# A PSUM bank of its own for the dilated attention's norm and transpose products, inside a recurrence stage

## The chip, the cores and the metric

The kernel runs on one core of a Trainium2 chip. The metric is the device time of one execution in microseconds; three runs of the kernel before gave a median of 2457.34 us (2457.04 to 2457.57). The core has five engines with a queue each, worked off in order: TensorE (PE, with its weight loads PEld), VectorE (DVE), ScalarE (ACT), GpSimd (POOL) and SyncE (SP), which here issues the DMAs. PSUM, where PE's products land, has eight banks of 128 partitions x 512 fp32 values.

## The reference

Two blocks on 512 tokens of width 1024. The first: x plus half a SwiGLU, then a mixer, then again half a SwiGLU. The mixer projects the normed x to an RWKV-7 branch, a dilated attention branch and two gates:

```python
p_rwkv, p_q, p_k, p_v, p_gate = _split_last(h @ w_in[l], (RWKV_COLS, ATTN_WIDTH, ATTN_WIDTH, ATTN_WIDTH, N_BRANCHES * D_MODEL))
y_a = rwkv7_time_mix(p_rwkv, ...)
y_b = dilated_attention(p_q, p_k, p_v, attn_q_norm[l], attn_k_norm[l])
g_a, g_b = _split_last(jax.nn.sigmoid(p_gate + b_gate[l]), (D_MODEL, D_MODEL))
merged = g_a * (y_a @ w_proj_rwkv[l]) + g_b * (y_b @ w_proj_attn[l])
x = x + merged @ w_out[l]
```

The RWKV branch is a recurrence over the tokens in 16 heads of 64, `state = state * w_t + (state @ a_t) b_t + v_t k_t`, with out = state @ r_t. The dilated attention has 12 heads in three groups; q and k are RMS-normed per head before it:

```python
q = rms_norm(heads(pq), q_gain) * (HEAD_DIM ** -0.5)
k = rms_norm(heads(pk), k_gain)
v = heads(pv)
```

The second block (two layers of a hybrid of MLA, GQA and a convolution, with a context) is not touched by the change.

## The kernel before, in words

Everything is fp32. A weight product is three matmuls over split operands (`mm3`, L623: whi*HH, whi*HL, wlo*HH); ACT makes whi from the DMA'd raw weights and DVE makes wlo (`wsplit`, L583). One 128 x 512 output tile over 8 k-slices is thus 24 matmuls into one PSUM bank, called prj in the stage below.

The change lies in the recurrence's stage, `rwkv` (L1185). There five streams of work run beside each other:

- `rw_chunks` (L1449), for each of 8 head pairs j, 8 chunks of 64 tokens one after the other. A chunk: po = AA x SV (PE, rows 0 to 63 and 64 to 127), copy pp <- po (ACT), pu = TB x pp (PE), copy SV <- pu (ACT), pS = Bt x SV (PE), a second product into po's rows 64 to 127 (PE), the state of the next chunk SV <- se + pS (DVE), and copy Og <- po (ACT), the chunk's output. After the eighth chunk a tail (`rw_tail`, L1496) norms the pair's output, with PE products py and pgg.
- `rw_solve` (L1403): for pair j the inverse of triangular blocks. AS is loaded from DRAM, 31 steps run on DVE (tiles pr and Tt), the result goes through DRAM into TB, DVE transposes AS <- TB, then PE products pZ and pW, and ACT copies TB <- pW. With that copy pair j's chunks may take pu. AS has one buffer.
- `rw_prep` (L1275): for pair j the decays, keys and the tiles AA, BB, Bt, SV. It has 13 PSUM tiles: pz, pa, pl, psk, prn, four of pA, pb, pv, two of pbt. Its tile AA has two buffers, so that DVE's AA <- pA for pair j waits for the last chunk of pair j-2.
- `rw_stream` (L1247): r, k and v projections, three prj tiles a pair, at most two pairs ahead.
- `rw_fill` (L1261): the attention's 18 q, k, v tiles (`qkv_steps`, L992), then 16 gate tiles. Each attention tile starts a chain (`qkv_chain`, L999): ACT copies fq <- prj (and, for q and k, squares it), which frees prj's bank. For q and k, PE makes ssq, the sums of squares; ten small DVE operations make the reciprocal root (dqx, dqi, drk, dqt); for k, ACT spreads it out, PE transposes it into bcq and DVE multiplies; the result is stored by qkT <- fq. For v, PE transposes into pt, ACT copies it and it is stored by vd <- fq. Only one chain is let in at a time (`qch`), and prj has two banks.

PSUM in this stage: pools "mm" (prj, 2 banks), "g" (2), "u" (pZ, pW, py, pgg; 1), "po" (2) and "us" (pu, pS; 1). All eight banks are in use.

The order of the work comes out of two steps. `drive` (L440) records which stream goes on next, by a clock with assumed durations, in which a tile waits for the earlier tile in its buffer (`alloc`, L295). Then the framework orders each engine's instructions by priority, which is the recorded order with shifts (`RW_LATE`, `RW_AHEAD`, L19 and L20: the chain's instructions come earlier, the projections' later, and twelve prj matmuls in a row stay together), hands out the buffers and sets the waits.

Of the kernel before, what the change touches and what calls it, by code (L numbers as in the profile page):

```python
# [7 lines left out]
F32 = mybir.dt.float32  # L8
# [5 lines left out]
P = 128  # L14
# [425 lines left out]
def drive(k, tasks):  # L440

    clk, plan, flags = k.clk, k.plan, k.flags
    live = {}
    n = 0

    def hint(x, y):
        x[3] = None
        if isinstance(y, tuple):  # L450
            x[3], y = y[:2], y[2]
        x[2] = clk.last
        if y.startswith("+"):
            y, x[2] = y[1:], 0.0
        x[5] = y.startswith("w")
        x[4] = y.lstrip("w")

    k.born = list(tasks)
    while live or k.born:
        for prio, y, g in k.born:  # L460
            live[n] = x = [prio, g, 0.0, None, "PE", False]
            hint(x, y)
            n += 1
        k.born = []
        if plan.recording:
            best = None
            for i, x in live.items():
                if x[5] and k.held:
                    continue
                r = x[2]  # L470
                if x[3] is not None:
                    w = flags.get(*x[3])
                    if w is None:
                        continue
                    r = max(r, w)
                s = clk.soon(x[4], r) + x[0]
                if best is None or s < best[0]:
                    best = (s, i)
            assert best is not None, ("tasks wait for one another", [(x[1].gi_code.co_name, x[3:]) for x in live.values()])
            i = best[1]  # L480
            plan.steps.append(i)
        else:
            i = plan.steps[plan.si]
            plan.si += 1
        x = live[i]
        assert x[3] is None or flags.get(*x[3]) is not None, "order of tasks"
        clk.last = 0.0
        late = k.late.get(x[1].__name__, 0)
        k.tc._tc.cur_priority += late
        try:  # L490
            y = next(x[1])
        except StopIteration:
            del live[i]
            continue
        finally:
            k.tc._tc.cur_priority -= late
        hint(x, y)
# [32 lines left out]
class K:  # L530
# [468 lines left out]
    def qkv_chain(self, g, u, i, p, k):  # L999
        nc, t1 = self.nc, self.t1  # L1000
        c = self.take("qch")
        yield self.need("qch", c, "ACT")
        v = p.rearrange("p (b t) -> p b t", b=4) if g == 0 else p.rearrange("p (t b) -> p b t", b=4)
        q = t1.tile([P, 4, P], F32, tag="fq0", name="fq0")
        nc.scalar.copy(q, v)
        if u == 2:
            self.free("rwmm", k)
            yield "PE"
            pt = self.rps["g"].tile([P, 4, P], F32, tag="g", name="pt")
            for b in range(4):  # L1010
                nc.tensor.transpose(pt[:, b], q[:, b], self.ident)
            yield "ACT"
            vt = t1.tile([P, 4, P], F32, tag="fq1", name="fq1")
            nc.scalar.copy(vt, pt)
            nc.sync.dma_start(self.vd[g][:, :, i * P:(i + 1) * P], vt)
            self.free("qch", c)
            return
        sq = t1.tile([P, 4, P], F32, tag="fq1", name="fq1")
        nc.scalar.square(sq, v)
        self.free("rwmm", k)  # L1020
        if u == 0:

            nc.sync.dma_start(self.qkT[g, 0][:, i], q.rearrange("p b t -> p (b t)"))
        yield "PE"
        ss = self.rps["g"].tile([P, 8], F32, tag="g", name="ssq")
        for b in range(4):
            nc.tensor.matmul(ss[:, 2 * b:2 * b + 2], sq[:, b], self.rcon["bd"][:, 0:128:64], start=b == 0, stop=True,
                             skip_group_check=True)
        yield "DVE"
        r = self.sm.tile([P, 8], F32, tag="drk", name="drk")  # L1030
        self.rstd(r, ss, 1.0 / 64, 1e-6, "dq")
        if u == 0:
            nc.vector.tensor_copy(self.RQ[:, g, :, 2 * i:2 * i + 2], r.rearrange("p (b h) -> p b h", h=2))
            self.free("qch", c)
            return
        yield "ACT"
        rnb = sq.rearrange("p b (h d) -> p (b h) d", d=64)
        nc.scalar.copy(rnb, r.unsqueeze(2).to_broadcast([P, 8, 64]))
        yield "PE"
        bc = self.rps["g"].tile([P, 4, P], F32, tag="g", name="bcq")  # L1040
        for b in range(4):
            nc.tensor.transpose(bc[:, b], sq[:, b], self.ident)
        yield "DVE"
        nc.vector.scalar_tensor_tensor(q, q, self.gg, bc, ALU.mult, ALU.mult)
        nc.sync.dma_start(self.qkT[g, 1][:, i], q.rearrange("p b t -> p (b t)"))
        self.free("qch", c)
# [138 lines left out]
    def rwkv(self, H, ya, tw, lad, gd):  # L1185
        nc, tc = self.nc, self.tc
        with ExitStack() as ctx:
            E = ctx.enter_context
            cp = E(tc.tile_pool(name="rc", bufs=1))
            self.t1 = E(tc.tile_pool(name="r1", bufs=1))  # L1190
            self.t2 = E(tc.tile_pool(name="r2", bufs=2))
            self.rps = {t: E(tc.tile_pool(name="rp" + t, bufs=b, space=PSUM))
                        for t, b in (("mm", 2), ("g", 2), ("u", 1), ("po", 2), ("us", 1))}
            self.scrA = [tc.dram_tile([2, 16, 32, 32], F32, name=f"scrA{j}") for j in range(8)]
            self.scrT = [tc.dram_tile([2, 16, 32, 32], F32, name=f"scrT{j}") for j in range(8)]
            self.rw = [dict() for _ in range(8)]
            o = PAR_COLS["a0"][0]
            self.a0h = cp.tile([P, 8], F32, name="a0h")
            nc.vector.tensor_scalar_mul(self.a0h, self.par_t[:, o:o + 8], 0.5)
            o = PAR_COLS["b_gate"][0]  # L1200
            self.bgh = cp.tile([P, 16], F32, name="bgh")
            nc.vector.tensor_scalar_mul(self.bgh, self.par_t[:, o:o + 16], 0.5)

            def seq(f, *a):
                s = (y for j in range(8) for y in f(j, *a))
                s.__name__ = f.__name__
                return s

            self.nb["rwmm"], self.nb["qch"] = 2, 1
            self.late = RW_LATE  # L1210
            drive(self, [
                (0, "PE", seq(self.rw_chunks, ya, gd)),
                (300, "PE", seq(self.rw_solve)),
                (600, "PE", seq(self.rw_prep, tw, lad)),
                (RW_PRIO["stream"], "PE", self.rw_stream(H)),
                (RW_PRIO["fill"], "PE", self.rw_fill(H)),
            ])
            self.late = {}
# [1290 lines left out]
```

## Time and profile before

| | |
|---|---|
| median of 3 runs | 2457.34 us |
| the profiled execution | 2463.02 us, its span 2461.2 us |
| PE busy, weight loads | 95%, 78% of the span |
| DVE, ACT, POOL busy | 70%, 41%, 8% |
| mean granted TensorE clock | 0.955 |
| the recurrence's stage | 392 to 1061 us of the span |

The profile is of one execution. Times count from the span's start. A tile is named by the program's name without its buffer number; "out<-in" says what an instruction writes and reads. PE's ends are modelled, so its starts are the better guide. Nearly all instructions carry the line of one recording helper (L320), so that they are told apart by their tiles. The granted clock is a share of full speed: 1.0 is 2.4 GHz, 0.5 is 1.2 GHz, and a figure between is a mixture over time.

### The profile page before, as it was taken

What the parts mean: (1) busy time and instruction counts of PE and PEld (TensorE: products, weight loads), DVE (VectorE), ACT (ScalarE), POOL (GpSimd) and SP (SyncE); (2) the same over time, 40 slices, a digit from 0 to 9 for tenths busy, and PEclk for the clock granted to TensorE, in tenths of its full rate; (3) what the DMA queues carried; (4) which work ended last, traced back from release to release, by engine and by line L of the source; (5) the groups of instructions that cost most, each with busy time, mean ns of one, the idle gap of its engine ahead of it and who ended that gap; (6) DMA issues with size and microseconds to landing.
All of it is one profiled execution on the core that took longest, in us unless ns stands there. A gap on an engine that the chain in (4) does not pass through costs nothing.

```text
span 2461.2 us, 33891 instructions
## 1 busy us (share of the span) xinstructions
PE 2347.4 (95%) x12556; PEld 1913.8 (78%) x12556; DVE 1733.4 (70%) x3620; ACT 1017.3 (41%) x1852; POOL 198.8 (8%) x202
## 2 busy tenths in 40 slices
PE   8999999999999999989989999999899999899997
PEld 7888887777777777758878888888778777678776
DVE  8888867675577656546668755656679976689866
ACT  4222234333333233345344542334446555355553
POOL 0000000011011110000001000000021210121110
PEclk9999999998799779989999999999999999899998
DMA  6545542333223224433333333243310222211121
GB/s 221 176 171 171 179 164 94 92 96 95 77 70 98 62 56 125 140 111 110 121 104 118 96 118 92 92 146 121 127 58 25 81 66 95 90 47 48 54 76 51
DMA packets 122199, 254.26 MB, mean 103 GB/s; under 512 B 39209, under 2 KB 54577, under 8 KB 121393
## 3 DMA queue, kind: packets, MB, share of 16 engines
q1 hardware_dynamic: 122032, 252.09, 32.5%
q8 instruction: 99, 1.62, 0.3%
q14 instruction: 68, 0.55, 0.1%
HBM read 222.07 MB, written 21.59 MB: 99 GB/s over the span
## 4 chain that ended last, share of the span: by engine, by line
PE 82%; DVE 9%; issue 3%; ACT 3%; POOL 2%; DMA 1%; SPq 0%; POOLq 0%; DVEq 0%; ACTq 0%
PE po L320 14%; PE prj L320 13%; PE pu L320 11%; PE pg L320 10%; PE pj L320 8%; PE pm L320 5%; PE pwo L320 4%; PE sc L320 2%; PE pt L320 2%; PE pA L320 2%; DVE X L320 1%; PE pkv L320 1%; PE pl L320 1%; PE ss L320 1%; DVE wlo L320 1%
## 5 line engine op out<-in xcount | busy, mean ns | idle before, releaser
L320 ACT CAST whi<-wraw 128x1024 fp32r<-128x1024 f32 (+4 forms) x330 | 324.9, 985 | 674.4 <-PE po L320 136.0
L320 DVE TENSOR_TENSOR wlo<-wraw,whi 128x512 fp32r<-128x512 f32 (+7 forms) x627 | 421.8, 694 | 103.1 <-ACT whi L320 92.5
L320 PE MATMUL prj<-HH,whi 128*128 128x512 f32 x464 | 199.3, 430 | 0.0
L320 PE MATMUL prj<-HH,wlo 128*128 128x512 f32 x464 | 192.5, 415 | 0.0
L320 PE MATMUL prj<-HL,whi 128*128 128x512 f32 x464 | 189.4, 408 | 0.0
L320 PE MATMUL pg<-HH,whi 128*128 128x512 f32 x352 | 139.2, 395 | 7.7 <-ACT HH L320 6.8
L320 PE MATMUL po<-FH,whi 128*128 128x512 f32 x352 | 139.0, 396 | 0.0
L320 PE MATMUL po<-FL,whi 128*128 128x512 f32 x352 | 139.0, 395 | 0.0
L320 PE MATMUL po<-FH,wlo 128*128 128x512 f32 x352 | 138.9, 395 | 0.0
L320 PE MATMUL pu<-HH,whi 128*128 128x512 f32 x352 | 138.7, 394 | 0.2 <-ACT whi L320 0.2
L320 PE MATMUL pg<-HL,whi 128*128 128x512 f32 x352 | 138.2, 393 | 0.0
L320 PE MATMUL pu<-HL,whi 128*128 128x512 f32 x352 | 137.5, 391 | 0.0
L320 PE MATMUL pu<-HH,wlo 128*128 128x512 f32 x352 | 135.0, 390 | 0.0
L320 PE MATMUL pg<-HH,wlo 128*128 128x512 f32 x352 | 134.9, 390 | 0.0
L320 PE MATMUL pj<-HH,whi 128*128 128x512 f32 (+1 forms) x304 | 124.6, 413 | 3.2 <-ACT HH L320 3.2
L320 ACT ACTIVATE pr<-sc,am 128x768 f32<-128x768 f32 (+1 forms) x120 | 97.9, 816 | 64.1 <-DVE am L320 58.3
L320 PE MATMUL pj<-HL,whi 128*128 128x512 f32 (+1 forms) x304 | 123.5, 407 | 0.0
L320 PE MATMUL pj<-HH,wlo 128*128 128x512 f32 (+1 forms) x304 | 122.0, 402 | 0.0
L320 DVE TENSOR_TENSOR ptl<-pt,pth 128x512 fp32r<-128x512 f32 x156 | 104.8, 683 | 23.1 <-ACT pth L320 21.5
L320 ACT CAST pth<-pt 128x512 fp32r<-128x512 f32 x156 | 89.6, 586 | 57.5 <-PE pt L320 56.7
L320 DVE TENSOR_REDUCE am<-sc 128x1 f32<-128x768 f32 (+1 forms) x120 | 100.6, 843 | 16.1 <-PE sc L320 15.6
L320 PEld LDWEIGHTS prj<-HH,whi 128*128 128x128 f32 x464 | 91.9, 198 | 23.3 <-issue 5.0
(745 smaller groups left out, 5633.1 us busy)
## 6 DMA issues: line engine op xcount, KB each, us to landing
wraw<-in_ffn_w SPq DMA_DIRECT2D x96, 512.0 KB, 3.4
wm<-in_l_mod SPq DMA_DIRECT2D x48, 512.0 KB, 4.4
wraw<-in_l_b SPq DMA_DIRECT2D x45, 512.0 KB, 3.3
wraw<-in_w_rkv SPq DMA_DIRECT2D x24, 512.0 KB, 4.1
wraw<-in_w_qkv SPq DMA_DIRECT2D x18, 512.0 KB, 3.4
wraw<-in_w_gate SPq DMA_DIRECT2D x16, 512.0 KB, 3.8
wraw<-in_ffn_w SPq DMA_DIRECT2D x16, 448.0 KB, 3.5
xd<-X SPq DMA_DIRECT2D x24, 256.0 KB, 2.1
```

Of the source, the lines that this page charges most:

```text
L320: r = real(*a, **kw)
```

## The change

The chain's three PSUM tiles go from pool "g" to a new pool "q" with one bank, and pool "po" goes from two banks to one. The total stays at eight banks.

```diff
@@ -1006,7 +1006,7 @@  qkv_chain
-            pt = self.rps["g"].tile([P, 4, P], F32, tag="g", name="pt")
+            pt = self.rps["q"].tile([P, 4, P], F32, tag="q", name="pt")
@@ -1022,7 +1022,7 @@
-        ss = self.rps["g"].tile([P, 8], F32, tag="g", name="ssq")
+        ss = self.rps["q"].tile([P, 8], F32, tag="q", name="ssq")
@@ -1037,7 +1037,7 @@
-        bc = self.rps["g"].tile([P, 4, P], F32, tag="g", name="bcq")
+        bc = self.rps["q"].tile([P, 4, P], F32, tag="q", name="bcq")
@@ -1190,7 +1190,7 @@  rwkv
             self.rps = {t: E(tc.tile_pool(name="rp" + t, bufs=b, space=PSUM))
-                        for t, b in (("mm", 2), ("g", 2), ("u", 1), ("po", 2), ("us", 1))}
+                        for t, b in (("mm", 2), ("g", 2), ("u", 1), ("po", 1), ("us", 1), ("q", 1))}
```

## Rows read from the trace of the kernel before

**Rows 1.** What touches tile pW: engine, operation, count, ns min/median/max, first and last start.
```profile
L320 ACT COPY TB<-pW x8: 558/574/577, 509.6 to 1027.8; 32x512 f32<-32x512 f32 x8
```
**Rows 2.** Windows between the TB<-pW copies, tile prj alone: busy and count by engine, PEclk, DMA.
```profile
509.60:586.70 77.10, 47.30 (x168) 32.08 (x168) 2.22 (x3) 5.51 (x9) 0.91 0.36 102
586.70:664.60 77.90, 39.76 (x135) 27.49 (x135) 1.47 (x2) 4.71 (x8) 0.82 0.28 76
664.60:739.20 74.60, 40.98 (x143) 27.28 (x143) 2.98 (x4) 4.93 (x8) 0.96 0.26 69
739.20:816.90 77.70, 44.01 (x167) 29.75 (x167) 3.72 (x5) 5.17 (x9) 0.92 0.34 96
816.90:883.30 66.40, 21.46 (x72) 14.65 (x72) 0.00 (x0) 1.68 (x3) 0.78 0.20 52
883.30:955.40 72.10, 37.10 (x145) 26.40 (x146) 0.00 (x0) 4.60 (x7) 0.86 0.37 99
955.40:1027.80 72.40, 54.66 (x205) 38.32 (x206) 0.00 (x0) 6.14 (x9) 0.95 0.35 109
1027.80:1061.10 33.30, 8.94 (x36) 6.39 (x36) 0.00 (x0) 1.36 (x2) 1.00 0.32 112
```
**Rows 3.** Timeline 834 to 885 (start, duration, engine, tiles, idle time before): one chain's wait.
```profile
835.62 1.38 PE L320 MATMUL pA<-AR,BK 64*128 64x128 f32 x10
...
839.27 0.59 ACT L320 COPY fq<-prj 128x512 f32<-128x512 f32 x1
...
862.31 0.69 DVE L320 TENSOR_TENSOR AA<-pA,c_rwmask 128x512 f32<-128x512 f32 x1 [0.44 <-PE po L320]
...
884.04 1.84 PE L320 MATMUL ssq<-c_bd,fq 128*128 128x2 f32 x8
```
**Rows 4.** Window 849 to 903, tile prj alone: PE, PEld, DVE, ACT, PEclk, DMA.
```profile
849.00:903.00 54.00, 0.47 (x2) 0.48 (x2) 0.00 (x0) 1.17 (x2) 0.62 0.22 53
```
**Rows 5.** Timeline: a chain that found a bank free, and the longest stall.
```profile
521.98 0.59 ACT L320 COPY fq<-prj 128x512 f32<-128x512 f32 x1 [2.23 <-PE prj L320]
...
525.00 0.95 PE L320 MATMUL ssq<-c_bd,fq 128*128 128x2 f32 x8
...
766.76 0.58 ACT L320 COPY fq<-prj 128x512 f32<-128x512 f32 x1
...
818.28 1.70 PE L320 MATMUL ssq<-c_bd,fq 128*128 128x2 f32 x8
```
**Rows 6.** Timeline 882 to 894 of SP: the DMAs that it issues, in order.
```profile
883.30 0.31 SPq L320 DMA_DIRECT2D AS<-scrA  x1
883.72 1.18 SPq L320 DMA_DIRECT2D AA<-AR  x2
891.11 0.34 SPq L320 DMA_DIRECT2D qkT<-fq  x1
891.49 1.36 SPq L320 DMA_DIRECT2D AS<-scrA  x3
```
**Rows 7.** Timeline 636 to 648 of DVE, around the transpose AS<-TB.
```profile
644.58 0.17 DVE L320 TENSOR_SCALAR dqx<-ssq 128x8 f32<-128x8 f32 x1 [2.16 <-PE ssq L320]
...
646.33 0.69 DVE L320 STREAM_TRANSPOSE AS<-TB 32x512 f32<-32x512 f32 x1
```
**Rows 8.** Timeline of PE: the tail's product pgg in the fourth and the sixth period.
```profile
804.51 2.06 PE L320 MATMUL pgg<-gd,lg 128*128 128x512 f32 x2
...
942.43 1.02 PE L320 MATMUL pgg<-gd,lg 128*128 128x512 f32 x2
```
**Rows 9.** Timeline: a chunk's output copy and the next chunk's first product, twice.
```profile
527.76 0.26 ACT L320 COPY Og<-po 64x128 f32<-64x128 f32 x1
...
530.07 0.33 PE L320 MATMUL po<-SV,AA 128*128 128x64 f32 x2
...
857.32 1.11 PE L320 MATMUL po<-SV,AA 128*128 128x64 f32 x4
857.43 0.26 ACT L320 COPY Og<-po 64x128 f32<-64x128 f32 x1 [1.39 <-PE po L320]
```

## The prediction

> **What bounds the kernel now.** I looked first at where the tiles of the change live. They live in the recurrence's stage, from 392 us to the last copy of a chunk at 1061 us, and nothing outside it is edited, so the question is what ends that stage. The second view was the small copy that ends each head pair's triangular solve, TB<-pW on ACT, once per pair, eight times from 509.6 to 1027.8 us [rows 1]. A pair's chunks need it, and the next pair's solve starts with it, because it frees the AS buffer. Its spacing is (1027.8 - 509.6) / 7 = 74.0 us, and after the last one 33 us of chunks remain. The third view cuts the stage at those eight copies [rows 2]. The reader is to see three columns there. The length of a period runs from 66.4 to 77.9 us. The count of projection matmuls (24 make one 512-column tile) is the fill of that period: 168, 135, 143, 167, 72, 145, 205, 36. The granted clock falls to 0.78 to 0.92 in some periods and stays at 0.95 or more in others. 0.78 is a mixture of the two levels, 2.4 and 1.2 GHz.
>
> So a period is set by a chain, not by one engine: copy TB, load AS, the solve's 31 steps on DVE, DMA out and in, pZ and pW on PE. A second chain lies beside it: this pair's chunks, their tail (py, pgg) and the one-bank pool "u", through which the next pair's pZ has to pass. Fill lengthens both. From the fifth period (72 matmuls, 3 tiles, 66.4 us) to the first (168, 7 tiles, 77.1 us) it costs (77.1 - 66.4) / 4 = 2.7 us a tile.
>
> **What the bank does now, and what the change removes.** Pool "g" has two banks, for the preparation's tiles and for the attention chain's ssq, bcq and pt. At 835.6 PE writes the preparation's two pA tiles, early. DVE can empty them only when the old AA buffer is free, at 862.3, released by a chunk's po [rows 3]. Until then both banks are held, and then the rest of the preparation passes through them. The chain's copy fq had been ready since 839.3, and its ssq comes at 884.0, 44.8 us later. Only one chain is let in at a time, so the next projection tiles can't be copied out of their two banks: between 849 and 903 us two projection matmuls start, and the clock is 0.62 [rows 4]. There are five such stalls, of 16 to 52 us; the longest is the one from 766.8 to 818.3. Where the banks were free, the same step took 3.0 us, from 522.0 to 525.0 [rows 5]. With a bank of its own I expect each stall to shrink to about that.
>
> The number of instructions stays: 12 times 8 for ssq, 6 times 4 each for bcq and pt, with their DVE, ACT and DMA steps. What changes is when they run. What a stall costs on the chains above:
> - SP's queue. At 883.3 the solve may load AS. One of four loads goes out, and the other three stand behind the chain's qkT store, which is issued at 891.1 [rows 6]. Of the 8 us between, the issue of those loads and of AA<-AR takes 2, so 6 are waiting. I take 5, because the attention's store will stand in front of other things instead.
> - DVE's queue. In the second period dqx waits for ssq at 644.6, 2.16 us idle, and the transpose AS<-TB that pZ needs is issued at 646.3, behind it and a dozen small operations [rows 7]. I take 3.
> - The clock. In the fourth period pgg's first half takes 2.06 us where at the full level it takes 1.02 [rows 8]. This level lasts over a dozen us up to the period's end, so 6 us are to be had; the fill that comes instead takes some: 4.
> - The first and third period's stalls, 21 and 16 us, hold nothing of the chain that I can read. 0 to 3 each; I take 3 for both.
>
> Sum: 5 + 3 + 4 + 3 = 15 us. What is late next is the tail and the bank "u". Against it: fill is moved, not removed. The fifth period takes some 4 tiles more, 4 x 2.7 = 11 us, and later periods get them back only while their solve chain doesn't end first. The fifth, with 3 tiles, still took 66.4 us. I take a loss of 4 there. The chain's ten DVE operations of 0.17 us [rows 7] now fall among the solve's steps, some 2 us a chain where DVE has no hole; that is in the 4.
>
> **What the change adds.** Og's copy has to end before the next chunk's first po product starts; before, that product took the other bank. Behind a waiting po on PE stand the fill and the preparation's products, and who waits for those is ACT's whi cast. Within a head pair there are 56 such places. With fill between, the copy starts at 527.76 and takes 0.26, and the next po comes at 530.07: 2.05 us to spare, cost nothing; the fill hides it. Without fill the next po starts at 857.32, before the copy does (857.43, 0.26 long), so it would move by some 0.42 us [rows 9]. In 11 of 56 places po starts before the copy ends or under 0.1 us later. So the lower end is 0, and the upper end, were all 56 tight, 56 x 0.42 = 23.5 us. I take 11 x 0.42 = 4.6, and of it 2, since most of them lie where the solve, not the chunks, ends the period. Between pairs the next pair's first po now goes early, and its next step waits for TB anyway: nothing.
>
> The Trainium skill speaks against this part: "Perfetto Trace Analysis", section Optimizing Tensor Performance, wants independent matmul groups to rotate through different banks, so that the eviction of one lies beside the next group's matmuls. By that rule every place would pay. By the rows most have fill there instead.
>
> Net: -15 + 4 + 2 = -9 us. The profiled execution took 2463.0 us, its span 2461.2, so it would become 2454; the runs' median, 2457.3, lies 5.7 below it, which gives 2448.
>
> **Rivals.**
> 1. PE, not the chain, is the bound, and the clock comes back. The clock lost over the eight periods [rows 2] is 77.1 x 0.09 + 77.9 x 0.18 + 74.6 x 0.04 + 77.7 x 0.08 + 66.4 x 0.22 + 72.1 x 0.14 + 72.4 x 0.05 = 58 us. If fill covers half of that, 29 us: 2428. For it speaks that the long stretch without fill is the one at 0.62; against it that the fill is then missing at the end of the stage, where the clock falls instead.
> 2. The stalls only hide: chain and tail end as late as before, and moved fill costs what it gives: 2457. For it speaks that the seven full periods differ by 11 us only, whatever their fill.
> 3. The eviction becomes the bound. Fill is used up early, and the chunks of the last three pairs run without it; also the whi casts on ACT can stand ahead of Og. Place: po behind Og. Price 0.42 us each. It outweighs a gain of 11 us once more than 26 of 56 places pay, and if all do the time is 2457 - 11 + 23.5 = 2470. This is the mechanism by which the rule above would hold. Against it: in the filled chunks po has 2 us to spare.
> 4. The fifth period becomes as long as the first, +10.7 us, since its tail and pZ now stand behind half tiles of fill, and the last periods give little back because their solve ends them: about 2464.
>
> **How the numbers follow.** Forecast 0.41, rivals 0.17, 0.20, 0.12, 0.10. The order of work comes from a recorded pass whose slots this change shifts too, so each case has some 8 us to either side. What can be told from no change is 0.2%, 5 us: below 2452.4 is faster. Faster: 0.41 x 0.85 + 0.17 + 0.03 = 0.55. Slower, above 2462.3: 0.12 x 0.8 + 0.10 x 0.6 + 0.05 = 0.21. Within: 0.24. The range runs from 2420, below rival 1 with its spread, to 2467, which leaves out the outer half of rival 3: under 2 in 10 together. The forecast's own range is 2440 to 2456.
>
> **What would show it.** Right: ssq within some 5 us of its fq copy everywhere; no stretch of 50 us without projection matmuls before the gate tiles end; the fifth period with 120 matmuls or more; AS loads no longer behind qkT by over 2 us; the last period without projection matmuls. Wrong: TB<-pW still 74 us apart (rival 2); PE idle before po with ACT Og as releaser, dozens of times (rival 3); the fifth period at 77 us and the sixth and seventh not shorter (rival 4); the stage's granted clock above 0.95 and 25 us gone (rival 1).

## The result, and the profile after

The kernel after took 2487.84 us (median of 4 runs, 2485.49 to 2498.37), the kernel before 2457.45 us beside it: a ratio of 1.0127, 95% interval 1.0101 to 1.0153. It is slower by 30 us, where 9 us faster had been forecast. A run over 1.5% above the fastest of its kernel counts as slow; below, e10 has one and e11 four, and medians, ratios and means leave them out.

The profiled execution took 2498.37 us against 2463.02. Of these 35 us, 33 lie in the recurrence's stage: the last Og copy ends at 1094.4 us instead of 1061.1. First the solve's closing copy on ACT (duration min/median/max, first and last start), which answers to [rows 1]:

```profile
L320 ACT COPY TB<-pW x8: 574/574/577, 505.2 to 1060.4; 32x512 f32<-32x512 f32 x8
```

The spacing went from 74.0 to (1060.4 - 505.2) / 7 = 79.3 us. The windows between these copies, tile prj alone (busy and count of PE, PEld, DVE, ACT, then granted clock and DMA), answer to [rows 2]:

```profile
505.20:591.80 86.60, 53.56 (x194) 36.81 (x194) 2.96 (x4) 6.09 (x10) 0.88 0.33 95
591.80:675.80 84.00, 50.89 (x179) 34.34 (x179) 3.71 (x5) 6.69 (x11) 0.91 0.28 78
675.80:755.90 80.10, 40.98 (x143) 28.38 (x143) 2.22 (x3) 3.21 (x5) 0.84 0.28 80
755.90:834.70 78.80, 38.84 (x120) 26.08 (x120) 2.22 (x3) 5.39 (x9) 0.80 0.25 68
834.70:916.30 81.60, 45.90 (x156) 31.59 (x156) 0.00 (x0) 4.30 (x7) 0.83 0.31 87
916.30:997.70 81.40, 55.13 (x193) 37.36 (x194) 0.00 (x0) 5.48 (x8) 0.90 0.35 100
997.70:1060.40 62.70, 27.62 (x108) 19.32 (x108) 0.00 (x0) 3.42 (x5) 0.93 0.37 110
1060.40:1094.40 34.00, 0.00 (x0) 0.00 (x0) 0.00 (x0) 0.00 (x0) 0.50 0.00 1
```

Six of seven full periods are longer, and the granted clock is lower in five of the eight. The fill now ends a period earlier: the last window has no projection matmul, and all of it runs at 0.50.

Yet the stalls are gone, as forecast: every ssq now comes within 4.4 us of its fq copy. In the timeline after, a chain's ssq comes 2.2 us behind its fq copy, where [rows 3] had 44.8:

```profile
853.09 0.59 ACT L320 COPY fq<-prj 128x512 f32<-128x512 f32 x1
...
855.27 0.95 PE L320 MATMUL ssq<-c_bd,fq 128*128 128x2 f32 x8
```

The list of waits of the stage (engine and tile that wait <- engine and tile waited for: us in total, times, longest) shows the DVE stall that answers to [rows 7] in the kernel before,

```profile
DVE dqx L320 <- PE ssq L320: 29.4, 11, 6.3
```

and after, beside the wait that the change was suspected to add:

```profile
DVE dqx L320 <- PE ssq L320: 6.4, 8, 1.3
PEld po L320 <- ACT Og L320: 6.0, 11, 0.9
```

In the period of [rows 6] SP now issues all four AS loads at once, with no qkT store between them. In the first two periods, though, a qkT store still stands between the loads (at 511.98 and 601.33) and holds the rest back by 6 and 9 us, and in the fifth all four come 3 us late, behind one. Before, two of the seven periods had a store between:

```profile
591.87 1.24 SPq L320 DMA_DIRECT2D AS<-scrA  x3
601.33 0.34 SPq L320 DMA_DIRECT2D qkT<-fq  x1
601.71 0.43 SPq L320 DMA_DIRECT2D AS<-scrA  x1
...
916.30 1.73 SPq L320 DMA_DIRECT2D AS<-scrA  x4
```

So where did the 33 us come from? Cut each pair at its first pu and its last Og copy. Between these two lies the **chunk stretch**; between a pair's last Og and the next pair's first pu lies the **gap** with tail, pZ and pW. The seven chunk stretches before the last sum to 393.7 us after and 324.8 before (+68.9); the seven gaps to 162.3 and 195.5 (-33.2); the stage's start and the last stretch make -4.0 and +1.6. The sum is +33.3. Fill moved with them: 37.9 tiles in those chunk stretches instead of 29.7, and 7.6 in the gaps instead of 13.8. Windows of two chunk stretches of the kernel before, tile prj alone:

```profile
587.69:636.35 48.66, 29.83 (x108) 20.25 (x108) 1.47 (x2) 3.03 (x5) 0.94 0.26 76
825.55:865.07 39.52, 15.69 (x60) 10.80 (x60) 0.00 (x0) 1.08 (x2) 0.83 0.15 48
```

and the same two after, with the gap ahead of each:

```profile
569.59:593.73 24.14, 8.46 (x26) 5.72 (x26) 0.75 (x1) 0.69 (x1) 0.74 0.37 88
593.73:655.87 62.14, 44.40 (x154) 29.79 (x154) 2.96 (x4) 4.92 (x8) 0.91 0.23 69
811.07:836.57 25.50, 7.74 (x23) 5.64 (x23) 0.74 (x1) 1.76 (x3) 0.77 0.40 98
836.57:893.95 57.38, 35.48 (x120) 24.76 (x120) 0.00 (x0) 3.61 (x6) 0.85 0.25 74
```

The timeline of one chunk after shows what a tile does there:

```profile
528.81 0.55 PE L320 MATMUL po<-SV,AA 128*128 128x64 f32 x4
...
530.35 0.26 ACT L320 COPY SV<-pu 64x128 f32<-64x128 f32 x1 [0.64 <-PE pu L320]
530.52 0.39 PE L320 MATMUL prj<-HH,whi 128*128 128x512 f32 x1
...
532.37 0.40 PE L320 MATMUL prj<-HH,wlo 128*128 128x512 f32 x1
532.70 0.45 PE L320 MATMUL pS<-SV,Bt 128*64 128x64 f32 x4
...
534.62 0.26 ACT L320 COPY Og<-po 64x128 f32<-64x128 f32 x1
```

pS could start when the copy into SV ends, at 530.61. It starts at 532.70, behind ten prj matmuls, and the next po, at 537.12, stands behind twelve more and an ssq. The chunk takes 8.3 us; without fill one takes 3.35 (26.8 us for the eight of the last pair in e1 below). So a tile costs over 5 us in a chunk stretch: its 24 matmuls, which follow each other at 0.228 us at the full clock, are hardly hidden at all. A least-squares line through the 80 chunk stretches of ten kernels (before, after and the first eight runs below) gives 5.8 us a tile and 0.44 us for each us at the lower clock, with 2.7 us of scatter; the 70 gaps give 5.2 us a tile and 0.61, with 3.5. Without the clock as a second term the same data give 5.2 and 3.4 us a tile. Expectations below use such prices, 5.1 to 5.3 and 3.2 to 3.4: part of the clock is in them.

The second part is the clock. After, it is at its lower level for 192 us of the stage, before for 133. Of the 59 us more, 33 lie in the seven chunk stretches and 32 in the last pair's, which has no fill any more; the gaps and the stage's start have 3 us less each. Windows after around one fall, all tiles:

```profile
904.00:908.00 4.00, 4.00 (x23) 3.41 (x22) 1.31 (x3) 2.79 (x4) 1.73 (x1) 1.00 0.57 136
908.00:912.00 4.00, 4.00 (x40) 2.32 (x39) 1.80 (x4) 0.60 (x1) 0.00 (x0) 1.00 0.08 24
912.00:916.00 4.00, 4.00 (x45) 2.43 (x42) 0.76 (x2) 1.26 (x2) 0.00 (x0) 0.52 0.57 193
```

PE is busy all the time by its modelled ends. What changes is what it does: 15 prj matmuls start in the first window, 2 in the second, none in the third, which holds the small products of tail, preparation and solve (pZ and pW of 32x32 among them). The clock falls at 912.2. Such a fall at the end of a gap meets the next pair's first chunk, whose group of fill then runs at the lower level. One in the timeline after:

```profile
594.50 0.26 ACT L320 COPY SV<-pu 64x128 f32<-64x128 f32 x1
596.07 0.77 PE L320 MATMUL prj<-HH,wlo 128*128 128x512 f32 x1
...
600.05 0.63 PE L320 MATMUL prj<-HH,wlo 128*128 128x512 f32 x1
600.61 0.69 PE L320 MATMUL pS<-SV,Bt 128*64 128x64 f32 x4
```

pS starts 5.85 us behind the copy that it needs, with ten prj matmuls 0.43 us apart in between.

### The profile page after: what moved, and what is told of

Read it like the earlier page. It is cut to its first block, busy times and chain, and to the rows that moved or that the text cites. A ratio compares the mean times of both kernels' runs of the same rounds, so it can differ in the third digit from the quotient of the medians.

```text
span 2496.5 us, 33959 instructions
## 1 busy us (share of the span) xinstructions
PE 2379.1 (95%) x12556; PEld 1931.6 (77%) x12556; DVE 1738.1 (70%) x3620; ACT 1018.0 (41%) x1852; POOL 191.3 (8%) x202
## 4 chain that ended last, share of the span: by engine, by line
PE 82%; DVE 10%; ACT 3%; POOL 2%; issue 2%; DMA 1%; SPq 0%; POOLq 0%; DVEq 0%; ACTq 0%
PE po L320 15%; PE prj L320 12%; PE pu L320 11%; PE pg L320 10%; PE pj L320 9%; PE pm L320 4%; PE pwo L320 4%; PE sc L320 3%; PE pt L320 2%; PE pA L320 2%; DVE X L320 1%; PE pl L320 1%; PE pkv L320 1%; PE ss L320 1%; DVE wlo L320 1%
## 5 line engine op out<-in xcount | busy, mean ns | idle before, releaser
L320 PEld LDWEIGHTS prj<-HH,wlo 128*128 128x128 f32 x464 | 93.7, 202 | 21.9 <-issue 1.0
```

The costliest lines, as they stand in the source:

```text
L320: r = real(*a, **kw)
```

## The experiments

For every run the mean clock c over the span t gives the time at the lower level, H = 2 x (1 - c) x t. The 75 runs of the kernel before beside these experiments went from 2446.81 us (c = 0.963) to 2475.26 (0.951) with one and the same order of instructions; their line has 0.40 us per us of H, and 185 runs of all kernels, each against its own mean, give 0.41. (The Trainium skill, "TensorE: Matmul & The Clock Gate", section HAM oscillation — how this bites in real kernels, takes half of the time at the low level as lost. The runs give less, 0.41; that PE would wait in part of this time anyway could explain it, but no run shows that.) With it each kernel's distance from before splits into 0.41 x the change of H and a **rest**, whose standard error is 0.2 to 1.2 us. "Chunk" and "gap" are fill tiles in the seven chunk stretches and gaps of the profiled run; H and rest are means over the runs counted.

| run | median us | ratio, 95% | chunk, gap | H | rest |
|---|---|---|---|---|---|
| before | 2457.45 to 2460.52 | | 29.7, 13.8 | 210 | 0 |
| after | 2487.84 | 1.0101 to 1.0153 | 37.9, 7.6 | 269 | +5.8 |
| e1 one po bank alone | 2494.64 | 1.0113 to 1.0165 | 34.5, 10.0 | 271 | +9.8 |
| e2 after, po in halves | 2492.79 | 1.0105 to 1.0167 | 37.9, 7.6 | 276 | +6.4 |
| e3 after, late fill | 2431.52 | 0.9859 to 0.9913 | 21.7, 19.0 | 157 | -5.9 |
| e4 before, late fill | 2451.67 | 0.9942 to 0.9989 | 18.3, 24.2 | 191 | -0.7 |
| e5 before, after's plan | 2472.12 | 1.0039 to 1.0094 | 33.0, 10.4 | 224 | +7.9 |
| e6 chain's bank from "g" | 2467.16 | 1.0004 to 1.0039 | 29.7, 12.8 | 210 | +5.5 |
| e7 after, single matmuls | 2461.81 | 0.9978 to 1.0031 | 14.8, 25.1 | 233 | -8.3 |
| e8 before, single matmuls | 2428.77 | 0.9848 to 0.9928 | 13.7, 28.7 | 159 | -8.9 |
| e9 after, RW_AHEAD 1000 | 2450.16 | 0.9926 to 0.9990 | 18.7, 24.8 | 187 | +1.6 |
| e10 one po bank, single | 2418.03 | 0.9807 to 0.9872 | 14.7, 27.2 | 134 | -8.6 |
| e11 before, RW_AHEAD 1000 | 2447.93 | 0.9907 to 0.9975 | 15.5, 26.0 | 166 | +2.9 |
| e12 as e9, po in halves | 2451.51 | 0.9958 to 1.0026 | 18.8, 24.7 | 200 | +0.9 |
| e13 e2 + 64 columns | 2491.39 | 1.0061 to 1.0177 | 38.5, 7.0 | 247 | +15.6 |
| e14 e2 + 256 columns | 2475.43 | 1.0032 to 1.0093 | 38.5, 7.0 | 213 | +14.0 |
| e15 e2 + 2 x 256 columns | 2495.44 | 1.0084 to 1.0188 | 40.4, 5.1 | 226 | +28.2 |
| e16 after, last pair | 2502.04 | 1.0114 to 1.0216 | 37.9, 7.6 | 274 | +15.7 |

### Is it the bank that po lost?

**e1**, the lost bank alone:

```diff
-  (("mm", 2), ("g", 2), ("u", 1), ("po", 2), ("us", 1))
+  (("mm", 2), ("g", 2), ("u", 1), ("po", 1), ("us", 1))
```

> The kernel before with the chunk-output pool cut from two banks to one, and nothing else: the chain stays in the two shared banks. Theory A (the fill's places): what made the kernel slower is the place that its fill tiles got in PE's instruction order, inside the stretches from a pair's first pu to its last Og instead of between them. Counted in the built order, the chunk stretches of pairs 2 to 8 hold 25.2 tiles before, 30.9 after and 28.9 here; by that, about two thirds of the 30 us: 2470 to 2480. Theory B (one chunk-output bank): the wait of po for the copy Og costs the 30 us by itself, 2480 to 2490. If neither of the two matters: 2457.

**e2**, the kernel after with two halves of the one bank:

```diff
+        if j == 0:
+            self.POB = self.rps["po"].tile([P, 2, 2, 64], F32, tag="po", name="po")
-            po = self.rps["po"].tile([P, 2, 64], F32, tag="po", name="po")
+            po = self.POB[:, c % 2]
```

> The kernel after, with two halves of the one chunk-output bank used in turn (chunk c writes half c mod 2), so that po no longer waits for the Og copy of the chunk before; the instruction order on every engine is that of the kernel after. Theory B (the wait of po for Og costs the 30 us): back to 2450 to 2460. Theory A (the order of the fill on PE costs them, whatever po waits for): 2482 to 2490.

One po bank alone, 2494.64 us, is as slow as the whole change, and a glance at e1 would convict it. e2 was to acquit po's wait, but it can't: its edit didn't take the wait away. In its last pair po starts 0.06 us behind the end of the Og copy and is released by it, as in the kernel after:

```profile
1056.02 0.26 ACT L320 COPY Og<-po 64x128 f32<-64x128 f32 x1 [1.39 <-PE po L320]
1056.34 1.11 PE L320 MATMUL po<-SV,AA 128*128 128x64 f32 x4 [0.35 <-ACT Og L320]
```

Its list of waits has the same PEld po <- ACT Og line as that of after, 6.0 us in 11 times. So e2 is the kernel after once more, at 2492.79 us, and says nothing of theory B.

What the wait costs can be read elsewhere. In e6 (below), whose po has two banks, the last pair also runs without fill and at the lower clock throughout, and there po starts before the copy:

```profile
1037.86 1.11 PE L320 MATMUL po<-SV,AA 128*128 128x64 f32 x4
1037.97 0.26 ACT L320 COPY Og<-po 64x128 f32<-64x128 f32 x1 [1.39 <-PE po L320]
...
1041.70 1.11 PE L320 MATMUL po<-SV,AA 128*128 128x64 f32 x4
```

A chunk takes 3.84 us there and 4.26 us in the kernel after: 0.42 us for the wait. After, po starts less than 0.1 us behind the copy in 9 of the 56 places, and seven of them are in this pair. That makes 3 to 4 us (an estimate: 7 to 9 times 0.42), not theory B's 30. What e1 changes besides is the built order (34.5 tiles in the chunk stretches instead of 29.7; H +61 us). It came out above theory A's 2470 to 2480, and 25 us of its distance from before go with the clock.

### Is it the place of the fill?

**e3** and **e4**, the same edit in the kernel after and in the kernel before:

```diff
-RW_LATE = {"rw_stream": 500, "rw_fill": 500, "qkv_chain": -1000}
+RW_LATE = {"rw_stream": 500, "rw_fill": 4000, "qkv_chain": -1000}
```

> The kernel after, with the fill's priority offset at 4000 instead of 500, so that the order gives the fill tiles later places: chunk stretches of pairs 2 to 8 hold 20.1 tiles instead of 30.9, and the gaps between them 22.2 instead of 7.6. Theory A: most of the 30 us comes back, or more, 2440 to 2460. Theory B: the single bank stays, 2480 to 2490.

> The kernel before with the same offset of 4000 for the fill: chunk stretches of pairs 2 to 8 hold 17.1 tiles instead of 25.2. Theory A: faster than 2457 by some 10 to 20 us, since fill leaves the chunk stretches here too. Theory B says nothing of it: 2457. If the gain of the run with the chain's bank and late fill is the fill's alone, this one gets it too; if the bank of its own is worth something once the fill is out of the way, this one is the slower of the two.

e3 keeps both banks of the change and goes from 2487.84 to 2431.52 us by a number that only moves fill, 8 us below theory A's range. Theory B falls: po has its one bank here too, and in none of the 56 places does it start less than 0.19 us behind the copy. e4 gained less than expected, 8 us, at 2451.67 with runs from 2436.52 to 2462.61; these lie on the clock's line (H from 156 to 217). The rest puts e3 ahead of e4 by 5.2 us.

**e5** has the banks of before when it runs, but records the plan with those of after. **e6** pays for the chain's bank out of "g":

```diff
+  # e5: before's pools when run, after's pools in the recorded pass; tag "q" there, "g" when run
+  (... ("po", 1), ("us", 1), ("q", 1)) if self.plan.recording else (... ("po", 2), ("us", 1))
+  # e6
+  (("mm", 2), ("g", 1), ("u", 1), ("po", 2), ("us", 1), ("q", 1))
```

> Banks of the kernel before (chain in the two shared banks, two banks for po) in the run, but the order of the generators' steps is recorded with the banks of the kernel after. So no bank is taken from anything that runs. By the built order the chunk stretches of pairs 2 to 8 hold 28.5 fill tiles instead of 25.2 and the gaps 10.5 instead of 13.9. In the runs so far a tile in a chunk stretch goes with 5.1 us, one in a gap with 3.2. Theory A (places of the fill): slower by 6 to 25 us, 2463 to 2482. Theory C (it needs the missing bank, as in the run with one po bank): 2457.

> The chain's bank of its own, paid by the shared pool (one bank instead of two); po keeps its two banks. Chunk stretches of pairs 2 to 8 hold 23.8 tiles, gaps 12.8. Theory A: near before, 2447 to 2470, and the preparation's tiles, now in one bank, are what could make it slower. Theory C (a missing po bank is what costs): 2445 to 2457, with the chain's stalls gone and no loss. If a bank of its own for the chain is what drags the fill into the chunk stretches: 2480 or more.

e5 is the plainest of all: no bank differs from before, the order does, and it takes 2472.12 us, in theory A's range and outside theory C's. So the order alone brings 12 of the 30 us; it isn't the order of after in full (33.0 tiles in the chunk stretches, not 37.9), and H rises by 14 us, not 59. In e6 the chunk stretches hold as much fill as before (29.7), H is the same, and 5.5 us are lost; of a gain by the bank nothing is seen, though what the lost bank of "g" costs is not separated from it.

### Fill spread thin, with and without the banks

**e7** (after), **e8** (before) and **e10** (one po bank) have RW_AHEAD = 0, so that matmuls of the fill are placed one by one; **e9** (after), **e11** (before) and **e12** (after, with e2's halves) have 1000:

```diff
-RW_AHEAD = 3000
+RW_AHEAD = 0      # e7, e8, e10;  1000 in e9, e11, e12
```

> The kernel after with the fill's matmuls placed one by one instead of in groups of four k-steps (twelve matmuls); nothing else. Chunk stretches of pairs 2 to 8 hold 15.0 tiles (30.9 after) and gaps 29.2 (7.6). Theory A: every tile that leaves a chunk stretch gives 5.1 us and costs 3.2 in a gap: below the run with the late fill (2431.5), 2410 to 2430. Theory that the number of po banks decides: 2480 or more.

> The kernel before with the same edit: chunk stretches of pairs 2 to 8 hold 13.3 tiles (25.2 before), gaps 29.0. Theory A: as fast as the run with the chain's own bank and single matmuls within 10 us, 2410 to 2435. If the bank of its own is worth something once the fill lies well, this one is the slower of the two by some 10 to 20 us, since it keeps the chain's stalls.

> The kernel after with RW_AHEAD at 1000 instead of 3000: groups of the fill's matmuls are held together less strongly, and the built order puts 15.9 tiles into the chunk stretches of pairs 2 to 8, 25.4 into the gaps and none behind the last Og (after: 30.9, 7.6, 0; the run with single matmuls: 15.0, 29.2 and 3.8 behind the end). Theory A, with its prices (5.3 us for a tile in a chunk stretch, 3.4 in a gap, 5.2 behind the end): as the run of before with single matmuls (2428.8) or a few us more, 2420 to 2440. If the single matmuls of the chain-bank kernel were slow for another reason than the tiles behind the end: 2455 or more again.

> The kernel before with one po bank and the fill's matmuls placed one by one: the order stands close to that of the run of before with single matmuls (chunk stretches 14.5 tiles against 13.3, gaps 27.3 against 29.0, 0.5 behind the end). Theory A: the po bank costs nothing by itself, 2425 to 2440. If one po bank costs its 35 us wherever the fill lies: 2460 or more.

> The kernel before with RW_AHEAD at 1000, the control of the chain-bank run with the same edit: chunk stretches 14.8 tiles, gaps 26.2, none behind the end. Theory A: 2425 to 2440. Against its partner it tells what the chain's own bank is worth in two orders whose fill lies alike: if the chain's stalls are worth the 15 us of the forecast, this one is 10 to 20 us the slower; if they only hide, the two are within 10 us.

> The chain-bank kernel with RW_AHEAD at 1000 and the two halves of the po bank in turn, in the same instruction order: the price of po's wait for Og where the chunks run tight and little fill lies between them. Theory A: equal to its partner within 6 us. Theory B: 5 to 23 us faster than its partner.

A chunk in the timeline of e10 (2418.03 us, the fastest of all, both given kernels included):

```profile
588.31 0.55 PE L320 MATMUL po<-SV,AA 128*128 128x64 f32 x4
...
589.78 0.44 PE L320 MATMUL pu<-pp,TB 64*64 64x64 f32 x4
590.15 0.50 PE L320 MATMUL prj<-HL,whi 128*128 128x512 f32 x1
590.49 0.40 PE L320 MATMUL prj<-HH,wlo 128*128 128x512 f32 x1
590.81 0.45 PE L320 MATMUL pS<-SV,Bt 128*64 128x64 f32 x4
591.19 0.44 PE L320 MATMUL po<-SV,TB 64*64 64x64 f32 x4
```

Two prj matmuls, not ten, stand between pu and pS, and pS starts 1.03 us behind pu; in the chunk of the kernel after above it was 2.88 (529.82 to 532.70).

e8 came out in its range, though not within 10 us of e7; e10 went below its range. e7 missed: 2461.81 where 2410 to 2430 had been expected, so the tile counts alone don't make the time. Two things were left out. It holds 3.8 tiles behind the last Og. And its H is 74 us above e8's, for the same rest (-8.3 and -8.9). One pair's chunk stretch in e7, tile prj,

```profile
723.00:770.67 47.67, 27.12 (x45) 11.75 (x45) 0.75 (x1) 1.27 (x2) 0.50 0.08 25
```

and the same pair's in e8:

```profile
728.98:757.52 28.54, 15.21 (x43) 6.84 (x43) 0.74 (x1) 0.68 (x1) 1.00 0.18 52
```

Nearly as many prj matmuls, 19 us apart, the clock at 0.50 throughout or at 1.00. e9, e11 and e12 spread over 33 us each from run to run, on the clock's line. e9 and e11 missed their ranges from above that way, so the worth of the chain's bank can't be read from their medians. The rests can be compared: chain's bank against none, e7 - e8 +0.6, e9 - e11 -1.3, e3 - e4 -5.2 us; one po bank against two, e10 - e8 +0.3. How well a rest repeats is seen in e9 - e12 +0.7 and after - e2 -0.6: e12, too, takes nothing away, since in e9 no po starts less than 0.19 us behind the copy. At equal clock, kernels with the chain's bank and without it lie 0 to 5 us apart, and the lost bank costs nothing that can be measured where no po comes right behind the copy. These are net figures: the fill of a pair of kernels lies alike only to within 1 to 5 tiles.

### Is the clock a cause, or only a companion?

**e13**, **e14**, **e15**: e2 with matmuls whose result nobody reads, into the free half of po's bank, n = 8, 8, 16 of w = 64, 256, 256 columns, written behind pZ and behind pW of every pair. On PE, e13 and e14 have one order.

```diff
+    def warm(self, n):
+        for _ in range(n):
+            self.nc.tensor.matmul(self.POW[:, 1, 0:w], self.wH[:, 0:128], self.wH[:, 0:w], start=True, stop=True, ...)
```

> The chain-bank kernel with po in two halves of one bank, and eight matmuls of 64 columns of no use (their result is read by nothing) into the free half of that bank behind pZ and behind pW in every pair. The control of the next run: same order on PE, a quarter of the columns. Fill stands as in the kernel after (chunk stretches of pairs 2 to 8 hold 32.0 tiles, gaps 7.0). All theories: near the run without them, 2485 to 2505.

> The same kernel with 256 columns in each of the extra matmuls, in the same order on PE. 128 of them over the eight pairs; a 128x512 product takes 0.216 us at full clock in these traces, so each takes 0.11 and they add at most 14 us of PE time, all on the path from solve to chunks. Theory K (the granted clock): many of the falls of the kernel after begin around pZ and pW, where PE does small products only; with 512 columns per stretch more, fewer falls or shorter ones, half-clock time in the stage lower by 40 to 80 us at 0.45 us each, less the 14: 5 to 25 us faster than the run with 64 columns, mean clock higher by 0.005 or more. Theory P (the place of the fill alone, clock only a companion): 5 to 14 us slower than the run with 64 columns.

> Sixteen extra matmuls of 256 columns behind pZ and pW each: at most 28 us of PE time added. Chunk stretches of pairs 2 to 8 hold 33.8 tiles, gaps 5.2, a little worse than in the two runs before. Theory K: fewer falls again, but the added time eats the gain: within 10 us of the run with eight. Theory P: 15 to 30 us slower than the run with 64 columns.

The matmuls don't run where they were written. From the second pair on, PE takes all sixteen of a pair together at the start of the gap, right behind the last Og copy of the pair before, some 15 us ahead of pZ in the case shown (e13 first, then e14):

```profile
560.50 1.97 PE L320 MATMUL po<-HH 128*128 128x64 f32 x16
563.35 2.16 PE L320 MATMUL po<-HH 128*128 128x256 f32 x16
```

So sixteen with four times the columns take only 0.2 us longer. (A 128x512 product takes 0.228 us in these traces at the full clock, not 0.216 as the expectation has it.) In the same places and order they made the kernel faster, by 15.2 us between the means (standard error 4.7). H fell by 33 us, which is 14 us by the line, and the rest by 1.6. In the profiled executions the gaps lost lower-clock time (59 to 17 us), while the chunk stretches gained some (60 to 72). That is theory K's side, though not at the place that it named. Its figure for H, 40 to 80, was too high, and the clock rose by 0.0064. Theory P, slower by 5 to 14, falls. The doubled dose, e15, costs 14 us more of rest and gives no clock back: 20 us slower than e14 and 4 slower than e13, outside both theories' figures; more of such matmuls gained nothing here.

**e16**, the same in the last pair's chunks, within po's own tile:

```diff
-            po = self.rps["po"].tile([P, 2, 64], F32, tag="po", name="po")
+            pw = self.rps["po"].tile([P, 2, 256], F32, tag="po", name="po")
+            po = pw[:, 0, 0:128].rearrange("p (h v) -> p h v", h=2)
+            # last pair: 3 of 128x256 into pw[:, 1] behind the first po products, 6 behind the second
```

> The kernel after in its own order, with three matmuls of 256 columns behind the first po products and six behind the second, in each of the eight chunks of the last pair only, where no fill stands and the clock is at its lower level from 1052 us on for 64.9 us; 72 matmuls, 8 us at full clock, beside waits of the chunk chain of over 2 us a chunk. Theory K: the clock stays at its upper level for most of this stretch, the eight chunks take 27 to 29 us instead of 32.1, and the mean clock rises by some 0.01 since the 64.9 us go: 5 to 15 us faster than after. Theory P: the same time or up to 8 us slower.

It was 14 us slower than after, and the clock stayed low; both theories' numbers are missed. The timeline (idle time before the instruction, and what ended it) shows why:

```profile
1063.09 0.69 PE L320 MATMUL po<-SV,TB 64*64 64x64 f32 x4
1063.71 1.65 PE L320 MATMUL po<-HH 128*128 128x256 f32 x6
1065.39 0.26 ACT L320 COPY Og<-po 64x128 f32<-64x128 f32 x1 [2.97 <-PE po L320]
1065.71 1.12 PE L320 MATMUL po<-SV,AA 128*128 128x64 f32 x4 [0.35 <-ACT Og L320]
```

The extra matmuls lie in po's tile, so the copies pp and Og wait for them too: they stand on the chunk chain, not beside it, and a chunk takes 6.59 us instead of 4.26. As a test of the clock the run is void. It also leaves the last pair's first po products out of what rows 64 to 127 sum up, since a start into the bank comes between po's two products; the instructions and waits stay. (The Trainium skill, "PSUM — Partial Sum Buffer", section Terms, has a start clear the marks of the bank's whole region. No trace here shows that by itself.)

## Why the prediction was wrong

- **The mechanism removed** was read rightly. ssq follows fq within a few us, the 50 us without projection matmuls are gone, the fifth period has 156 of them and the last has none: four of the five signs named as "right" are there. The fifth is there in part only: in two of seven periods a qkT store still stands between the AS loads, as often as before, so that over the stage as a whole SP's term of 5 us has nothing to show for it.
- **The 15 us of gain** don't show: at equal clock, kernels with and without the chain's own bank lie 0 to 5 us apart in three pairs. This agrees with rival 2, that the stalls mostly hid, but no run takes the stalls alone away, and none of the four terms was measured singly.
- **"Fill is moved, not removed ... I take a loss of 4 there"** is the step that failed. It priced a tile at 2.7 us wherever it lies, and asked only whether the fifth period would grow. The stall had kept fill out of PE's way. Without it the fill ran ahead: 8.2 tiles more in the chunk stretches, at 5.8 us each, and 6.2 fewer in the gaps, at 5.2. By these two lines that is 48 - 32 = 16 us at equal clock. The last pair's chunks have one tile less (6 us), and the first pair's begin 4 us earlier, which leaves 6; the runs' rest is 5.8. The lines' scatter is wider than this agreement. Rival 4 (tail and pZ behind half tiles, 2464) had the mechanism, for one period where it was six.
- **The clock, "+4"**, had the wrong sign, and it is the larger part. The forecast had more fill bring the clock back in one period. Instead H rose from 210 to 269 us, which is 24 of the 30 us. In the profiled executions the chunk stretches have 33 us more at the lower clock and the last pair's chunks 32. These run without fill now, and that goes with it in all 18 traces: the eight kernels without a projection matmul in the last pair's chunks have 10 to 50 us at the lower clock there, the ten with 1 to 3 tiles at most 4. That end had been seen: rival 1 names it as what speaks against a clock that comes back, but the sum has no term for it.
- **po's wait**, taken at 2 us with 23.5 as the upper end, was about right in kind and size: where it stands it costs the 0.42 us foretold, and it stands in the last pair without fill, 3 us in all, which are then part of the rest of 5.8. The lines that answer to [rows 9]:

```profile
1064.72 0.26 ACT L320 COPY Og<-po 64x128 f32<-64x128 f32 x1 [1.39 <-PE po L320]
1065.04 1.12 PE L320 MATMUL po<-SV,AA 128*128 128x64 f32 x4 [0.35 <-ACT Og L320]
```

  po starts 0.06 us behind the copy's end. The Trainium skill's rule about rotating banks ("Perfetto Trace Analysis", section Optimizing Tensor Performance), and rival 3 with it, show up in these chunks alone, not in every place.
- **That the order would shift** was put at 8 us to either side. The experiments moved the time from 41 us below before (e10) to 35 above it (e1). That range should have been the widest term of all.

Left open: which of the falls of the clock belongs to which group of fill. e13 and e14 show that columns in the gap change H, not how the 59 us of H came about one by one. Open too: what the chain's bank is worth by itself, with every other instruction in its place.

## What to carry to other kernels

In a kernel whose work order is built by a scheduler, a stall may be what holds cheap filler back: before removing one, ask where the released work goes, and price it there by the chain it will stand in, not by an average. Split a time difference by the granted clock of the runs before looking for waits; here two runs of one kernel differ as much as two kernels. And look in the trace whether an experiment did what it was made for: e2's wait stood where it had been, and e14's matmuls ran 15 us ahead of their place. e1 alone would have convicted the wrong bank; what cleared it was the price of the wait, read from the same chunks with one bank and with two.

## What was not expected of the hardware

The clock fell while PE showed no idle time by its modelled ends, in stretches of small products (4.00 of 4.00 us busy from 908 to 912, and the fall at 912.2), and one kernel's runs differ by up to 33 us (e9, 2435.88 to 2469.07) with their mean clock (0.969 to 0.954) and nothing else changed in the program. Extra columns that nobody reads made a kernel faster (e14 against e13, 15 us) and cost almost no time of their own (0.2 us for sixteen matmuls).
